# The half-sized products' first accumulator in two parts: one 512-column matmul for both operand parts, and PSUM pools by phase

## The chip, the cores and the metric

The kernel runs on one core of a Trainium2 chip. The time is the device time of one execution in microseconds; below, "before" is the kernel without the change.

## What is computed

A decoder trunk of two layers over one sequence of 512 tokens with 1024 features, in float32: a feed-forward layer (FFN), a mixer and a second FFN in each layer. The change touches the four FFNs alone. Each is a SwiGLU of 2816 columns behind an RMS norm:

```python
def swiglu(h, w13, w2):
    gate, up = jnp.split(h @ w13, 2, axis=-1)
    return (jax.nn.silu(gate) * up) @ w2
for l in range(DEPTH):
    x = x + 0.5 * swiglu(rms_norm(x, ffn1_norm[l]), ffn1_w13[l], ffn1_w2[l])
    ...
    x = x + 0.5 * swiglu(rms_norm(x, ffn2_norm[l]), ffn2_w13[l], ffn2_w2[l])
```

## The kernel before

**Data.** The activations are kept with features on the 128 partitions and the 512 tokens along the free dimension. Every float32 operand of TensorE is split in two parts of a narrower type, `hi` and `lo`; a product is the sum of three matmuls, `hi·xh`, `hi·xl` and `lo·xh` (L388 to L390), with the weights stationary. A weight block is loaded by DMA (`w_raw`, or `w_a` for a block and `w_s` for a sum of blocks), ACT casts its high part (`w_hi`, L85), and DVE subtracts for the low part (`w_lo`, L89).

**One FFN** (`ffn`, L353). The 22 column tiles of gate and up are done in thirds of 8, 8 and 6 tiles (`THIRDS`). The first tiles of a call (6, 4, 0 and 4 in the four calls, `PLAIN`) are plain products of 512 columns; the others are taken two at a time by `pair` (L370), 37 pairs in all. After each third come its "down" products `pd`, eight groups of 24 (or 18) matmuls of 512 columns, which read the pair's results `ah` and `al`.

**A pair** is a 2 by 2 block product of gate and up tiles against two halves of 256 tokens, done with seven half-sized products instead of eight. The operands' combinations of token halves are made before (`hh`, `hl`: seven forms each, high and low part); the weights' sums `s1` to `s4` are added by DVE (L114). The seven products f0 to f6 go one after the other into three PSUM banks, X, Z and Y, which are drained on the way:

- f0 into X, copied to `e[:, 0]` by ACT (L391)
- f1 into Z, added by DVE (L397)
- f2 into X on top of f0, copied to `e[:, 1]` by ACT (L395)
- f3 into Y, copied to `e[:, 2]` by ACT (L393)
- f4 into X, subtracted by DVE (L399)
- f5 into Y, subtracted by DVE (L401)
- f6 into X; ACT applies silu to it straight from PSUM (L404), DVE multiplies (L406)

So X is written four times in a pair, and each time the PE may go on writing it only when the drain of the time before is done. Each product is 24 matmuls of 256 columns: 2 column halves, 4 blocks of features, 3 parts. The silu of the other three quarters is L403, their multiplication L405; L411 (ACT) and L412 (DVE) split the result into `ah` and `al`.

**Order.** The program is recorded with a scheduler that fixes each engine's order ahead of time; every engine then takes its instructions strictly in that order, and waits at an instruction whose operands are late. Within an FFN `w_hi` and `w_lo` have five buffers each: the parts of a product's weights can be made only when PE has finished with the product five places before. All PSUM tiles come from one pool of eight banks, `psum` (L161). `mm` (L200) issues each matmul.

## Time and profile before

| | us |
|---|---|
| median of 3 runs (1862.65 to 1864.32) | 1862.82 |
| the profiled execution | 1862.41 |
| its span, first to last instruction | 1860.7 |
| TensorE busy | 1836.7 (99%) |
| VectorE (DVE) busy | 1357.0 (73%) |
| ScalarE (ACT) busy | 919.2 (49%) |

The profiled execution lies 0.4 us under the median. The span is the profiled time less 1.7 us that lie around it. Busy shares are averages over the whole program; what limits a stage is read from that stage alone. A row of the timeline gives an instruction's start and its duration; instructions of one engine overlap, so the distance between two starts (the pitch) is what one costs the engine, and the duration is what a waiting engine sees. A row of the groups by line gives the busy time, the mean duration in ns, and the idle time before the instructions with what ended it.

### The profile page before, as it was taken

What the parts mean: (1) busy time and instruction counts of PE and PEld (TensorE: products, weight loads), DVE (VectorE), ACT (ScalarE), POOL (GpSimd) and SP (SyncE); (2) the same over time, 40 slices, a digit from 0 to 9 for tenths busy, and PEclk for the clock granted to TensorE, in tenths of its full rate; (3) what the DMA queues carried; (4) which work ended last, traced back from release to release, by engine and by line L of the source; (5) the groups of instructions that cost most, each with busy time, mean ns of one, the idle gap of its engine ahead of it and who ended that gap; (6) DMA issues with size and microseconds to landing.
All of it is one profiled execution on the core that took longest, in us unless ns stands there. A gap on an engine that the chain in (4) does not pass through costs nothing. (4 is left out here: it accounts for less than half of the span.)

```text
span 1860.7 us, 27263 instructions
## 1 busy us (share of the span) xinstructions
PE 1836.7 (99%) x11040; PEld 1628.6 (88%) x11040; DVE 1357.0 (73%) x1678; ACT 919.2 (49%) x1282; POOL 123.5 (7%) x165
## 2 busy tenths in 40 slices
PE   9999999999999999999999999999999999999999
PEld 7889989787789899897789999898776789899897
DVE  8958757698878486576799667575799779577483
ACT  6525425477555254354555335254588655345251
POOL 1000000032000000000100000000345300000000
PEclk9999999999999999999999999999999999999999
DMA  6223523222414134232463324234476421425131
GB/s 227 89 81 93 146 63 108 69 91 79 151 54 157 50 112 136 67 104 79 159 204 122 111 86 138 66 105 145 124 197 165 140 88 59 144 74 159 54 111 59
DMA packets 73117, 207.87 MB, mean 112 GB/s; under 512 B 7584, under 2 KB 17056, under 8 KB 72480
## 3 DMA queue, kind: packets, MB, share of 16 engines
q1 hardware_dynamic: 72704, 205.81, 36.2%
q8 instruction: 86, 1.41, 0.3%
q10 hardware_dynamic: 288, 0.32, 0.1%
q14 instruction: 39, 0.32, 0.0%
HBM read 189.85 MB, written 16.25 MB: 111 GB/s over the span
## 5 line engine op out<-in xcount | busy, mean ns | idle before, releaser
L85 ACT CAST w_hi<-w_raw 128x1024 fp32r<-128x1024 f32 (+1 forms) x165 | 165.7, 1007 | 270.3 <-PE pdffn L201 82.4
L85 ACT CAST w_hi<-w_s 128x1024 fp32r<-128x1024 f32 x148 | 155.2, 1050 | 246.5 <-PE pdffn L201 105.4
L89 DVE TENSOR_TENSOR w_lo<-w_raw,w_hi 128x1024 fp32r<-128x1024 f32 (+3 forms) x191 | 218.1, 1145 | 71.8 <-ACT w_hi L85 65.7
L201 PE MATMUL pXffn<-hhffn,w_hi 128*128 128x256 f32 x832 | 235.8, 283 | 0.3 <-ACT effn L391 0.3
L201 PE MATMUL pXffn<-hhffn,w_lo 128*128 128x256 f32 x832 | 235.6, 283 | 0.0
L201 PE MATMUL pXffn<-hlffn,w_hi 128*128 128x256 f32 x832 | 235.6, 283 | 0.0
L201 PE MATMUL pdffn<-ahffn,w_hi 128*128 128x512 f32 x592 | 230.9, 390 | 0.3
L201 PE MATMUL pdffn<-alffn,w_hi 128*128 128x512 f32 x592 | 230.8, 390 | 0.0
L201 PE MATMUL pdffn<-ahffn,w_lo 128*128 128x512 f32 x592 | 230.5, 389 | 0.0
L89 DVE TENSOR_TENSOR w_lo<-w_s,w_hi 128x1024 fp32r<-128x1024 f32 x148 | 180.7, 1222 | 32.3 <-ACT w_hi L85 31.9
L85 ACT CAST w_hi<-w_a 128x1024 fp32r<-128x1024 f32 x111 | 116.6, 1050 | 167.5 <-PE pdffn L201 70.2
L89 DVE TENSOR_TENSOR w_lo<-w_a,w_hi 128x1024 fp32r<-128x1024 f32 x111 | 135.6, 1222 | 36.1 <-ACT w_hi L85 36.0
L201 PEld LDWEIGHTS pXffn<-hhffn,w_hi 128*128 128x128 f32 x832 | 159.8, 192 | 1.1 <-ACT effn L391 0.7
L201 PEld LDWEIGHTS pXffn<-hlffn,w_hi 128*128 128x128 f32 x832 | 159.8, 192 | 0.3
L201 PEld LDWEIGHTS pXffn<-hhffn,w_lo 128*128 128x128 f32 x832 | 159.8, 192 | 0.0
L455 DVE SCALAR_TENSOR_TENSOR x<-pdffn,x 128x512 f32<-128x512 f32 x72 | 49.8, 691 | 141.2 <-PE pdffn L201 141.2
L201 PEld LDWEIGHTS pdffn<-ahffn,w_hi 128*128 128x128 f32 x592 | 111.2, 188 | 24.6 <-ACT ahffn L411 1.8
L201 PEld LDWEIGHTS pdffn<-alffn,w_hi 128*128 128x128 f32 x592 | 111.2, 188 | 24.2 <-DVE alffn L412 1.1
L201 PEld LDWEIGHTS pdffn<-ahffn,w_lo 128*128 128x128 f32 x592 | 111.2, 188 | 22.7
L201 PE MATMUL pYffn<-hhffn,w_lo 128*128 128x256 f32 x416 | 117.8, 283 | 0.0
L201 PE MATMUL pYffn<-hhffn,w_hi 128*128 128x256 f32 x416 | 117.8, 283 | 0.0
L201 PE MATMUL pYffn<-hlffn,w_hi 128*128 128x256 f32 x416 | 117.8, 283 | 0.0
(1146 smaller groups left out, 4631.4 us busy)
## 6 DMA issues: line engine op xcount, KB each, us to landing
w_a<-in_ffn_s SPq DMA_DIRECT2D x148, 512.0 KB, 3.7
w_raw<-in_ffn_w SPq DMA_DIRECT2D x90, 512.0 KB, 4.5
w_raw<-in_ffn_w SPq DMA_DIRECT2D x32, 384.0 KB, 3.3
w_raw<-in_w_in SPq DMA_DIRECT2D x16, 512.0 KB, 3.6
qp<-qd SPq DMA_DIRECT2D x14, 512.0 KB, 6.1
w_raw<-in_w_out SPq DMA_DIRECT2D x8, 512.0 KB, 3.7
w_raw<-in_w_k SPq DMA_DIRECT2D x8, 512.0 KB, 3.6
w_raw<-in_w_v SPq DMA_DIRECT2D x8, 512.0 KB, 3.7
```

Of the source, the lines that this page charges most:

```text
L85: nc.scalar.copy(out=hi[:, cs], in_=raw[:, cs])
L89: eng.tensor_tensor(out=lo[:, cs], in0=raw[:, cs], in1=hi[:, cs].bitcast(F32), op=ALU.subtract)
L201: return nc.tensor.matmul(o, l, r, start=start, stop=stop, skip_group_check=True)
L455: nc.vector.scalar_tensor_tensor(out=x[m], in0=pd, scalar=0.5, in1=x[m], op0=ALU.mult, op1=ALU.add)
```

## The change

For each feature block and column half the X products take `hi·xh` and `hi·xl` in one matmul of 512 columns: the moving operand is two pieces of 256, and `hh` becomes one tile that holds high and low part (`[P, 2, 7, 256]`). Their results stand side by side, so X is now two banks, one for each column half, with a high and a low part of 256 columns that have yet to be added; `lo·xh` still goes, in 256 columns, onto the high part. Z and Y stay as they were. The drains of X change with it:

- f0 and f2: ACT copies the low part (L384 of the changed kernel), then DVE adds the high part (L385); before, one ACT copy
- f4: two DVE operations (L425, L426); before, one
- f6: ACT negates the low part into `e` (L430), DVE takes the high part off (L431), and silu (L434) and product (L436) read SBUF; before, they read PSUM

PSUM pools are opened by phase: in an FFN four single banks and two two-bank tiles for X (`ps=4, px=2`), elsewhere eight single banks. The plain products' gate and up share a two-bank tile for every other column tile.

```diff
-    pp = ctx.enter_context(tc.tile_pool(name="pp", bufs=8, space=PSUM))
...
-        return pp.tile([P, S], F32, tag="ps", name=name)
-
-
-    cur = SimpleNamespace(stack=[], names=[])
+        return cur.pp.tile([P, S], F32, tag="ps", name=name)
+
+    def psum2(name):
+
+        return cur.pp.tile([P, 2, S], F32, tag="px", name=name)
+
+    def open_psum(name, **bufs):
+
+        if cur.pp is not None:
+            cur.pp.pool_ctx.__exit__(None, None, None)
+        ctxm = tc.tile_pool(name=name, bufs=2, space=PSUM, reuse_waits="tile")
+        cur.pp = Pool(ctxm.__enter__(), bufs)
+        cur.pp.pool_ctx = ctxm
...
-        hi = cur.ht.tile([P, 7, HS], F32R, tag="hh", name=f"hh{name}{j}")
-        lo = cur.ht.tile([P, 7, HS], F32R, tag="hl", name=f"hl{name}{j}")
+        t = cur.ht.tile([P, 2, 7, HS], F32R, tag="hh", name=f"hh{name}{j}")
+        hi, lo = t[:, 0], t[:, 1]
...
+        open_psum(f"pf{n}{l}", ps=4, px=2)
...
+        def add2(o, p, q):
+            nc.scalar.copy(out=o, in_=q)
+            nc.vector.tensor_tensor(out=o, in0=p, in1=o, op=ALU.add)
...
-                    banks[bank] = psum(f"p{bank}{n}{l}{i}")
+                    banks[bank] = (psum2 if bank == "X" else psum)(f"p{bank}{n}{l}{i}")
                 ps = banks[bank]
+                if bank == "X":
+                    xh, xl = (ps[:, :, k * HS:(k + 1) * HS] for k in range(2))
                 for c in range(2):
-                    o = ps[:, c * HS:(c + 1) * HS]
+                    o = ps[:, c] if bank == "X" else ps[:, c * HS:(c + 1) * HS]
                     for j in range(KT // 2):
                         ws = slice(c * S + j * P, c * S + j * P + P)
-                        xh, xl = hn[j][0][:, form], hn[j][1][:, form]
-
-                        mm(o, hi[:, ws], xh, new and c == 0 and j == 0, False)
-                        mm(o, hi[:, ws], xl, False, False)
-                        mm(o, lo[:, ws], xh, False, j == KT // 2 - 1)
-
+                        if bank == "X":
+                            mm(o, hi[:, ws], hn[j][:, :, form], new and j == 0, False)
+                            mm(o[:, 0:HS], lo[:, ws], hn[j][:, 0, form], False, j == KT // 2 - 1)
+                            continue
+                        th, tl = hn[j][:, 0, form], hn[j][:, 1, form]
+
+                        mm(o, hi[:, ws], th, new and c == 0 and j == 0, False)
+                        mm(o, hi[:, ws], tl, False, False)
+                        mm(o, lo[:, ws], th, False, j == KT // 2 - 1)
...
                if f == 0:
-                    nc.scalar.copy(out=e[:, 0], in_=ps)
+                    add2(in2[0], xh, xl)
+                elif f == 1:
+                    nc.vector.tensor_tensor(out=c11, in0=ps, in1=c11, op=ALU.add)
+                elif f == 2:
+                    add2(in2[1], xh, xl)
                 elif f == 3:
-                    nc.scalar.copy(out=e[:, 2], in_=ps)
-                elif f == 2:
-                    nc.scalar.copy(out=e[:, 1], in_=ps)
-                elif f == 1:
-                    nc.vector.tensor_tensor(out=e[:, 0], in0=ps, in1=e[:, 0], op=ALU.add)
+                    nc.scalar.copy(out=c22, in_=ps)
                 elif f == 4:
-                    nc.vector.tensor_tensor(out=e[:, 2], in0=ps, in1=e[:, 2], op=ALU.subtract)
+                    nc.vector.tensor_tensor(out=in2[2], in0=xh, in1=in2[2], op=ALU.subtract)
+                    nc.vector.tensor_tensor(out=in2[2], in0=xl, in1=in2[2], op=ALU.add)
                 elif f == 5:
-                    nc.vector.tensor_tensor(out=e[:, 1], in0=ps, in1=e[:, 1], op=ALU.subtract)
-            ps = banks["X"]
-            nc.scalar.activation(out=e[:, 0:3, 0:HS], in_=e[:, 0:3, 0:HS], func=AF.Silu)
-            last_silu.append(nc.scalar.activation(out=e[:, 3, 0:HS], in_=ps[:, 0:HS], func=AF.Silu, scale=-1.0))
-            nc.vector.tensor_tensor(out=e[:, 0:3, 0:HS], in0=e[:, 0:3, 0:HS], in1=e[:, 0:3, HS:S], op=ALU.mult)
-            nc.vector.scalar_tensor_tensor(out=e[:, 3, 0:HS], in0=ps[:, HS:S], scalar=-1.0, in1=e[:, 3, 0:HS], op0=ALU.mult, op1=ALU.mult)
+                    nc.vector.tensor_tensor(out=c21, in0=ps, in1=c21, op=ALU.subtract)
+                elif f == 6:
+                    nc.scalar.mul(in2[3], xl, -1.0)
+                    nc.vector.scalar_tensor_tensor(out=in2[3], in0=xh, scalar=-1.0, in1=in2[3], op0=ALU.mult, op1=ALU.add)
+
+            for b in (slice(0, 3), slice(3, 4)):
+                last_silu.append(nc.scalar.activation(out=e[:, b, 0:HS], in_=e[:, b, 0:HS], func=AF.Silu))
+            for b in (slice(0, 3), slice(3, 4)):
+                nc.vector.tensor_tensor(out=e[:, b, 0:HS], in0=e[:, b, 0:HS], in1=e[:, b, HS:S], op=ALU.mult)
...
-                pg, pu = psum(f"pg{n}{l}{i}"), psum(f"pu{n}{l}{i}")
+                if i % 2 == 0:
+                    pgu = psum2(f"pgu{n}{l}{i}")
+                    pg, pu = pgu[:, 0], pgu[:, 1]
+                else:
+                    pg, pu = psum(f"pg{n}{l}{i}"), psum(f"pu{n}{l}{i}")
```

The lines of the operations move: the copy of f3 is L423 after the change, the drains of f1 and f5 L419 and L428, the splits L441 and L442, `mm` L213.

**Where the order moves on PE.** In the names, `effn1018` is the drained tile of the pair of column tiles 18 and 19 in the first FFN, call 0 (`ffn1`, `0`, `18`); `pXffn1020` is bank X of the pair behind it. Before, PE goes from f1 of pair 1020 (Z) straight to f2 (X):

```order
L201 MATMUL pZffn1020_2965<-hhffn103_420,w_lo78_2827 128x256
L201 MATMUL pXffn1020_2935<-hhffn100_365,w_hi79_2859 128x256
L201 MATMUL pXffn1020_2935<-hlffn100_366,w_hi79_2859 128x256
L201 MATMUL pXffn1020_2935<-hhffn100_365,w_lo79_2860 128x256
L201 MATMUL pXffn1020_2935<-hhffn101_380,w_hi79_2859 128x256
L201 MATMUL pXffn1020_2935<-hlffn101_381,w_hi79_2859 128x256
```

After the change, at the same place:

```order
L213 MATMUL pZffn1020_2766<-hhffn103_420,w_lo78_2648 128x256
L213 MATMUL pYffn1020_2822<-hhffn100_368,w_hi80_2704 128x256 x2
L213 MATMUL pYffn1020_2822<-hhffn100_368,w_lo80_2705 128x256
L213 MATMUL pYffn1020_2822<-hhffn101_382,w_hi80_2704 128x256
L213 MATMUL pXffn1020_2743<-hhffn100_368,w_hi79_2673 128x512
L213 MATMUL pXffn1020_2743<-hhffn100_368,w_lo79_2674 128x256
L213 MATMUL pXffn1020_2743<-hhffn101_382,w_hi79_2673 128x512
L213 MATMUL pXffn1020_2743<-hhffn101_382,w_lo79_2674 128x256
L213 MATMUL pXffn1020_2743<-hhffn102_406,w_hi79_2673 128x512
```

Four matmuls of f3 (Y; a row with x2 is two) now stand between f1 and f2, and f2 takes two matmuls for a feature block and column half where it took three. Of the sixteen matmuls of the next pair's f0, six stand further ahead, between the products f3 to f6 of pair 1018 (five in f3's place, behind 20 of its 24, and one before f6), so that ten are left between f6 and Z; before, all of f0 stood there. In the first pair of a stage Z is followed by one matmul of f3 instead of four.

**Where the order moves on DVE.** The end of pair 1018 and the beginning of pair 1020, before:

```order
L89 TENSOR_TENSOR w_lo80_2891<-w_s3_80_2888,w_hi80_2890 128x1024
L405 TENSOR_TENSOR effn1018_2696<-effn1018_2696 128x3x256
L89 TENSOR_TENSOR w_lo81_2932<-w_s1_79_2855,w_hi81_2931 128x1024
L406 SCALAR_TENSOR_TENSOR effn1018_2696<-pXffn1018_2701,effn1018_2696 128x256
L412 TENSOR_TENSOR alffn1018_2923<-effn1018_2696,ahffn1018_2922 128x512
L412 TENSOR_TENSOR alffn1019_2927<-effn1018_2696,ahffn1019_2926 128x512
L89 TENSOR_TENSOR w_lo82_2962<-w_a22_77_2792,w_hi82_2961 128x1024
L397 TENSOR_TENSOR effn1020_2930<-pZffn1020_2965,effn1020_2930 128x512
```

And after the change:

```order
L436 TENSOR_TENSOR effn1018_2531<-effn1018_2531 128x3x256
L89 TENSOR_TENSOR w_lo81_2740<-w_s1_79_2669,w_hi81_2739 128x1024
L431 SCALAR_TENSOR_TENSOR effn1018_2531<-pXffn1018_2536,effn1018_2531 128x512
L89 TENSOR_TENSOR w_lo82_2763<-w_a22_77_2613,w_hi82_2762 128x1024
L436 TENSOR_TENSOR effn1018_2531<-effn1018_2531 128x256
L385 TENSOR_TENSOR effn1020_2738<-pXffn1020_2743,effn1020_2738 128x512
L442 TENSOR_TENSOR alffn1018_2731<-effn1018_2531,ahffn1018_2730 128x512
L442 TENSOR_TENSOR alffn1019_2735<-effn1018_2531,ahffn1019_2734 128x512
L419 TENSOR_TENSOR effn1020_2738<-pZffn1020_2766,effn1020_2738 128x512
```

The drain of f6 (L431) now stands between two weight parts, the product of the last quarter (L436) behind both, and the drain of f0 of the next pair (L385), which was not on DVE before, behind all of them; the splits (L412, now L442) come after it.

**And the middle of the pair, DVE after the change:**

```order
L114 TENSOR_TENSOR w_s1_79_2669<-w_a21_77_2611,w_a22_77_2613 128x1024
L89 TENSOR_TENSOR w_lo77_2618<-w_a11_77_2609,w_hi77_2617 128x1024
L385 TENSOR_TENSOR effn1018_2531<-pXffn1018_2536,effn1018_2531 128x512
L114 TENSOR_TENSOR w_s2_79_2671<-w_s1_79_2669,w_a11_77_2609 128x1024
L89 TENSOR_TENSOR w_lo78_2648<-w_a12_77_2615,w_hi78_2647 128x1024
L114 TENSOR_TENSOR w_s3_80_2702<-w_a11_77_2609,w_a21_77_2611 128x1024
L425 TENSOR_TENSOR effn1018_2531<-pXffn1018_2536,effn1018_2531 128x512
L114 TENSOR_TENSOR w_s4_83_2792<-w_s2_79_2671,w_a12_77_2615 128x1024
L426 TENSOR_TENSOR effn1018_2531<-pXffn1018_2536,effn1018_2531 128x512
L89 TENSOR_TENSOR w_lo79_2674<-w_s2_79_2671,w_hi79_2673 128x1024
```

The drain of f2 (L385) stands behind `w_lo77`, and the two of f4 (L425, L426) have a weight sum between them.

**And the first pair behind plain products** (column tiles 4 and 5 of `ffn2`, call 0), DVE after the change:

```order
L89 TENSOR_TENSOR w_lo132_4851<-w_s1_130_4778,w_hi132_4850 128x1024
L380 TENSOR_TENSOR effn203_4840<-effn203_4840 128x512
L385 TENSOR_TENSOR effn204_4849<-pXffn204_4854,effn204_4849 128x512
L89 TENSOR_TENSOR w_lo133_4874<-w_a22_128_4707,w_hi133_4873 128x1024
L339 TENSOR_TENSOR affn203l_4846<-effn203_4840,affn203h_4845 128x512
L419 TENSOR_TENSOR effn204_4849<-pZffn204_4877,effn204_4849 128x512
L114 TENSOR_TENSOR w_s4_134_4903<-w_s2_130_4780,w_a12_128_4709 128x1024
L89 TENSOR_TENSOR w_lo135_4936<-w_a11_135_4927,w_hi135_4935 128x1024
L89 TENSOR_TENSOR w_lo134_4906<-w_s4_134_4903,w_hi134_4905 128x1024
L385 TENSOR_TENSOR effn204_4849<-pXffn204_4854,effn204_4849 128x512
```

L380 multiplies gate and up of the plain tile 3, and L339 splits it; the drain of f0 (L385) stands behind the first and that of f1 (L419) behind the second. f0's was ACT's before, and PE's f2 waited for it; now 15 matmuls of f3 stand ahead of f2.

## Rows read from the trace of the kernel before

**Rows 1.** The page: busy time of each engine, granted clock in 40 slices.

```profile
PE 1836.7 (99%) x11040; PEld 1628.6 (88%) x11040; DVE 1357.0 (73%) x1678; ACT 919.2 (49%) x1282; POOL 123.5 (7%) x165
...
PEclk9999999999999999999999999999999999999999
```

**Rows 2.** Stretches of the pair stages: busy time (instructions) of each engine.

```profile
core 0: us, PE busy (x) PEld busy (x) DVE busy (x) ACT busy (x) POOL busy (x), PEclk, DMA share, GB/s
...
562.60:603.70 41.10, 40.79 (x337) 40.37 (x336) 35.84 (x40) 23.04 (x30) 0.00 (x0) 1.00 0.50 168
647.30:727.90 80.60, 80.60 (x673) 80.60 (x672) 63.45 (x66) 42.13 (x53) 0.00 (x0) 1.00 0.45 131
...
sum 746.40, PE 746.09 PEld 745.58 DVE 591.81 ACT 395.61 POOL 0.00; mean PE 62.17 PEld 62.13 DVE 49.32 ACT 32.97 POOL 0.00
```

**Rows 3.** Timeline of PE: plain products of 512 columns, then the first pair's X.

```profile
73.11 0.39 PE L201 MATMUL puffn<-h_7h,w_hi 128*128 128x512 f32 x1
...
73.79 0.28 PE L201 MATMUL pXffn<-hhffn,w_hi 128*128 128x256 f32 x1
...
76.66 0.28 PE L201 MATMUL pZffn<-hhffn,w_hi 128*128 128x256 f32 x1
```

**Rows 4.** Timeline of PE around the end of an X product, in a later pair.

```profile
1107.12 0.28 PE L201 MATMUL pXffn<-hhn,w_lo 128*128 128x256 f32 x1
1107.24 0.28 PE L201 MATMUL pXffn<-hhn,w_hi 128*128 128x256 f32 x1
```

**Rows 5.** Timeline of ACT, the same place.

```profile
1107.37 1.05 ACT L85 CAST w_hi<-w_s 128x1024 fp32r<-128x1024 f32 x1 [1.09 <-PE pXffn L201]
1108.32 0.38 ACT L404 ACTIVATE effn<-pXffn 128x256 f32<-128x256 f32 x1
```

**Rows 6.** Timeline of DVE, the same place.

```profile
1108.45 1.23 DVE L89 TENSOR_TENSOR w_lo<-w_s,w_hi 128x1024 fp32r<-128x1024 f32 x1 [0.79 <-ACT w_hi L85]
1109.59 0.42 DVE L406 SCALAR_TENSOR_TENSOR effn<-pXffn,effn 128x256 f32<-128x256 f32 x1
```

**Rows 7.** Timeline of DVE: an operation of 512 columns from PSUM and the next.

```profile
562.13 0.68 DVE L366 TENSOR_TENSOR effn<-puffn,rs_n 128x512 f32<-128x512 f32 x1
562.73 1.22 DVE L89 TENSOR_TENSOR w_lo<-w_s,w_hi 128x1024 fp32r<-128x1024 f32 x1
```

**Rows 8.** Timeline of DVE: the first pair of a stage of two.

```profile
569.67 0.69 DVE L367 TENSOR_TENSOR effn<-effn 128x512 f32<-128x512 f32 x1
...
572.01 0.69 DVE L397 TENSOR_TENSOR effn<-pZffn,effn 128x512 f32<-128x512 f32 x1
...
587.11 0.42 DVE L406 SCALAR_TENSOR_TENSOR effn<-pXffn,effn 128x256 f32<-128x256 f32 x1
587.44 1.22 DVE L89 TENSOR_TENSOR w_lo<-w_s,w_hi 128x1024 fp32r<-128x1024 f32 x1
```

**Rows 9.** Timeline of PE at the wait of the same stage.

```profile
568.24 0.28 PE L201 MATMUL pZffn<-hhffn,w_lo 128*128 128x256 f32 x1
568.77 0.39 PE L201 MATMUL pXffn<-hhffn,w_hi 128*128 128x256 f32 x1 [0.25 <-ACT effn L391]
568.99 0.28 PE L201 MATMUL pXffn<-hlffn,w_hi 128*128 128x256 f32 x1
```

**Rows 10.** Timeline of PE's weight loads at that wait.

```profile
568.12 0.19 PEld L201 LDWEIGHTS pZffn<-hhffn,w_lo 128*128 128x128 f32 x1
568.76 0.19 PEld L201 LDWEIGHTS pXffn<-hhffn,w_hi 128*128 128x128 f32 x1 [0.45 <-ACT effn L391]
```

**Rows 11.** Timeline of ACT at that wait.

```profile
568.15 0.56 ACT L391 COPY effn<-pXffn 128x512 f32<-128x512 f32 x1
```

**Rows 12.** Groups by line: the drain of f4.

```profile
L399 DVE TENSOR_TENSOR effn<-pXffn,effn 128x512 f32<-128x512 f32 x37 | 25.4, 687 | 9.1 <-PE pXffn L201 9.0
```

**Rows 13.** Timeline of PE in the attention: matmuls with an operand in two pieces.

```profile
1377.01 0.28 PE L201 MATMUL z<-sph,ntri 128*128 128x256 f32 x1
1377.13 0.28 PE L201 MATMUL z<-spl,ntri 128*128 128x256 f32 x1
```

More of the change, by code (lines that the diff above doesn't have):

```diff
@@ L157, in trunk @@
     wp = ctx.enter_context(tc.tile_pool(name="wp", bufs=3))
-    pp = ctx.enter_context(tc.tile_pool(name="pp", bufs=8, space=PSUM))
     dp = ctx.enter_context(tc.tile_pool(name="dp", bufs=8, space=DRAM))
     def psum(name):
-        return pp.tile([P, S], F32, tag="ps", name=name)
-    cur = SimpleNamespace(stack=[], names=[])
+        return cur.pp.tile([P, S], F32, tag="ps", name=name)
[7 more added lines that the diff above has]
+        cur.pp.pool_ctx = ctxm
+    cur = SimpleNamespace(stack=[], names=[], pp=None)
     def temp(tag, name, dt=F32, bufs=2, shape=None):
@@ L190, in phase_ffn @@
         close_pools()
-        cur.ht = open_pool("ht", hh=4, hl=4)
+        cur.ht = open_pool("ht", hh=4)
         cur.ep = open_pool("ep", e=2)
@@ L196, in phase_mix @@
         close_pools()
+        open_psum(f"pm{len(cur.names)}", ps=8)
         cur.hp = open_pool("hp", bh=8, bl=8, ch=8, cl=8)
@@ L350, in normed @@
         nc.vector.scalar_tensor_tensor(out=lo[:, 6], in0=b22, scalar=-1.0, in1=hi[:, 6].bitcast(F32), op0=ALU.mult, op1=ALU.subtract)
-        return hi, lo
+        return t
     def ffn(n, l, ht, g, rs, after, full=False, hn=None):
+        open_psum(f"pf{n}{l}", ps=4, px=2)
         r, queue, nf = None, [], PLAIN[n, l]
@@ new lines, in pair @@
+                        th, tl = hn[j][:, 0, form], hn[j][:, 1, form]
+                        mm(o, hi[:, ws], th, new and c == 0 and j == 0, False)
+                        mm(o, hi[:, ws], tl, False, False)
+                        mm(o, lo[:, ws], th, False, j == KT // 2 - 1)
+                c11, c21, c22, c12 = (e[:, k] for k in range(4))
+                in2 = [t.rearrange("p (c t) -> p c t", c=2) for t in (c11, c21, c22, c12)]
+                if f == 0:
+                    add2(in2[0], xh, xl)
[3 more added lines that the diff above has]
+                    add2(in2[1], xh, xl)
+                elif f == 3:
+                    nc.scalar.copy(out=c22, in_=ps)
@@ L462, in x_tiles @@
         return halves, [halves[m // 4][:, m % 4] for m in range(KT)]
+    open_psum("pw", ps=1)
     x2, x = x_tiles("x")
@@ L662, in trunk @@
     cur.tp = open_pool("tk")
+    open_psum("pk", ps=8)
     r3 = None
@@ L1017, in trunk @@
     ffn("ffn2", 1, h5, G_FFN2[1], n5.rstd, lambda m, t: nc.sync.dma_start(out[:, m], t))
+    cur.pp.pool_ctx.__exit__(None, None, None)
     close_pools()
```

## The prediction

> **What bounds the kernel now.** I began with the page: PE is busy for 1836.7 of 1860.7 us at full granted clock, DVE for 73% [rows 1]. That names PE, but a share over the program hides stages, so the stretches of the pair stages come next. There PE never stops: 746.09 of 746.40 us, and in a stage of four pairs 80.60 of 80.60, with DVE at 63.45 [rows 2]. The one kind with waits is the stage of two pairs behind plain products, 41.10 us [rows 2] where two pairs of 168 matmuls need 40.3: 0.8 of waits. So PE's own time bounds a pair, and what saves matmul time saves time as long as no wait takes its place. The third view, the timelines, gives prices: on PE for the matmuls, on ACT and DVE for the drains that PE will wait for.
>
> **What is saved.** A 512-column matmul costs (73.79 - 73.11) / 3 = 0.2267 us [rows 3]. A 256-column one costs 80.60 / 672 = 0.1199 [rows 2], and the first X product agrees: 24 in 76.66 - 73.79 = 2.87 [rows 3]. Merging two saves 2 x 0.1199 - 0.2267 = 0.013. There are 37 pairs x 4 X products x 8 = 1184 such merges: **15.6 us**, 0.42 per pair (20.15 becomes 19.73). An X product falls from 2.88 to 2.77.
>
> **What is added.** On DVE four operations of 128x512 per pair (L385 twice, the second of f4, L431 in place of nothing). One costs 0.60 in a row of others [rows 7], so 2.4 us per pair. A pair has 11 operations of 128x1024 at 1.14 [rows 6], three drains at 0.60, 0.87 + 0.33 for the two products (the second from [rows 8]) and two splits at 0.60: 16.7 us, now 19.1 of some 19.9. DVE still has room, but little, so what counts is the place of each drain in its strict order. On ACT one copy more per pair lies in idle time (42.13 of 80.60 busy, [rows 2]): nothing.
>
> **The length of a drain.** Call T the moment at which the next matmul could start after an X product. The last matmul of a product starts at 1107.12, so T is 1107.24 [rows 4]. The cast of the freed weight buffer starts at T + 0.13, and the next ACT operation 0.95 later [rows 5]. Its w_lo starts at T + 1.21 and the DVE operation behind it at T + 2.35 [rows 6]. A drain put there takes 0.69 [rows 12] and some 0.05 until PE knows (a copy ends at 568.15 + 0.56 = 568.71 [rows 11], PE loads at 568.76 [rows 10]). So a drain behind one w_lo releases PE at **T + 3.09**.
>
> A late release costs more than its lateness. At the wait that before has, X could have started at 568.24 + 0.12 = 568.36 and started at 568.77; its next matmul came 0.22 later instead of 0.12 [rows 9]. I charge each restart 0.10, and a release less than 0.10 ahead of its matmul the difference.
>
> On this the Trainium skill speaks too. "TensorE: Matmul & The Clock Gate", section "Step-by-step: what each phase is for", says that PE pulls weight loads ahead of running matmuls. By that rule a restart would find its weights loaded and cost nothing, which would take some 4 us off the waits below (about 45 restarts). The trace disagrees at this place: the load starts with the release, 0.64 after the load ahead of it [rows 10].
>
> **Place by place**, with the order shown above:
>
> 1. *f0 of a later pair, before f2.* DVE takes w_lo81 at T + 1.21 (T: end of the pair before), L431 to 2.95, w_lo82 to 4.09, L436 to 4.42, then the drain: 4.42 + 0.69 + 0.05 = T + 5.16. PE has ten matmuls of f0 (1.73), 24 of Z (2.88), four of Y (0.48): T + 5.09. Cost 0.07 + 0.10 = 0.17. 37 pairs less 12 first ones less two priced in 4: 23 x 0.17 = 3.9.
> 2. *f0 of a first pair.* T + 3.09 against Z and one Y, 3.00: 0.19. Nine stages of three or four pairs: 1.7.
> 3. *f2 and f4 elsewhere.* In a middle pair f2's drain is released at 3.09 against 20 matmuls of Y and five of f0, 3.32: no cost. f4's second drain stands behind s4: 0.20 + 0.60 + 1.14 + 0.69 + 0.05 = 2.68 against 3.00: none. In four of the nine first pairs a w_lo stands between f4's two drains, 3.09 again against 3.00 to 3.1, and f2's is just in time: 0.28 together; in the other five some 0.1. The last pair of a third of six tiles has one filler instead of five: 0.1 in each of four. Sum 1.1 + 0.5 + 0.4 = 2.0.
> 4. *The two stages behind plain products.* DVE is late there: f1's add starts at 572.01, Z's last matmul at 568.24 [rows 8, 9]. f0's drain now stands behind L380, that is at 569.67 + 0.60 = 570.27 [rows 8], and releases at 571.01; PE gets there at 568.25 + 15 x 0.12 = 570.05. Cost 1.06. The matmuls of the next pair's f0 that are pulled ahead then wait for their w_hi (T + 0.13 + 1.05 + 0.05 of f2) and w_lo: 0.25 and 1.02. With 0.4 in the second pair 2.7, less the 0.8 that is there now: 1.9 each, 3.8.
> 5. *Matmuls that wait for weights in the middle of a pair*: a w_lo is there at T + 1.21 + 1.22 + 0.05 = 2.48 against 20 x 0.12 + 0.23 = 2.63. Nothing, with 0.15 to spare. The pools by phase and the shared gate and up tile change no wait in a pair; cover is the whole phase before. Nothing.
>
> Sum of waits 3.9 + 1.7 + 2.0 + 3.8 = **11.4**, against 15.6: net -4.2. From the profiled execution 1862.4 that is 1858.2; the median of the runs stands 0.4 higher, so 1858.6, **1859 us**.
>
> The sum is a difference of near equals. The unknown prices: a DVE add that reads two banks in pieces has no row. From below it is the row I take, 0.60 and 0.69 [rows 7, 12]; nothing excludes a little more, so from above I take the 0.42 that 256 columns cost [rows 8] twice, 0.84. I take the lower, since the data are the same size. The merged matmul is bounded below by 0.2267 and above by two single ones, 0.24; I take the lower, by the nearest row: in the attention, matmuls of 2 x 128 columns from an operand in two pieces start 0.12 apart [rows 13], as contiguous ones do.
>
> **Rivals.**
>
> *All drains are hidden* (chance 0.22). Place 1 lacks only 0.17 of 5.1 us; if DVE's steps are 3% shorter, or the release comes as soon as the drain's write does, places 1 to 3 vanish and 1862.4 - 15.6 + 3.8 = 1851 is left, 1847 if the backlog does no harm either. (Were the restarts alone free, 1859 - 4 = 1855, inside the forecast's own band.) For it: PE waits for nothing now. Against: the steps were measured without gaps.
>
> *DVE becomes the bound* (0.22), the one that ends slower. Place: f0's drain, then f2's and f4's. If an add costs 0.75 instead of 0.60, six of them put DVE at 20.0 us a pair, place 1 grows by 0.3, and the spare 0.13 to 0.2 of f2, f4 and the pulled-ahead w_lo is gone: some 0.3 to 0.4 more in each of 37 pairs, 11 to 15 us, 1870 to 1874. It decides from about 0.1 us more per add, where place 1 alone eats what is left of the saving.
>
> *An operand in two pieces is slow* (0.06). If the merged matmul took 0.24, the saving would be 0 and the waits some 8 (covers are longer): 1871. [Rows 13] speak against it. [...]
>
> *It cancels* (0.08): the waits take all of the 15.6, as they do where each release is 0.1 later than I have it; 1860 to 1865.
>
> **Numbers.** My forecast has 0.42. 0.2%, 3.7 us, is about what a measurement of this kernel can tell from no change, so faster means below 1859.1. The forecast, 1854 to 1864, is split there: 0.24 faster, 0.18 same. With 0.22 of the first rival, faster is 0.45; same is 0.18 + 0.08 and a little of the rivals' edges, 0.28; slower 0.22 + 0.06 less those edges, 0.27. The range takes in the first rival down to 1849 and the slow ones up to 1873.
>
> **What would show it.** 9856 matmuls; X products at 2.77 from start to start; idle PE time before X with DVE's L385 as its releaser, about 0.1 to 0.2 each in later pairs, 1 us at the two stages behind plain products; DVE at 19 of 20 in a pair. Stages of four pairs should take 79.6 to 80.0 us instead of 80.60. Wrong would be idle PE before f4 or f6 in middle pairs, L385 longer than 0.7, or a pitch of 0.24 in the merged matmuls.

## The result, and the profile after

| | before | after |
|---|---|---|
| median, us (3 runs of before from above and one more beside the change; 4 runs of after) | 1863.57 | 1873.37 |
| lowest and highest | 1862.65 to 1865.53 | 1872.99 to 1874.07 |
| ratio with its 95% interval | | 1.0054 [1.0041, 1.0066] |
| the profiled execution, and its span | 1862.41, 1860.7 | 1874.07, 1872.2 |

The change makes the kernel slower by 9.8 us. The forecast, 1859 and rather faster, has the wrong sign, and the time lies 0.4 us above the range.

Page of after: busy time of each engine, granted clock in 40 slices. These answer to [rows 1].

```profile
PE 1840.5 (98%) x9856; PEld 1567.0 (84%) x9856; DVE 1442.0 (77%) x1826; ACT 941.9 (50%) x1319; POOL 122.6 (7%) x165
...
PEclk9999999999999999999999999999999999999999
```

The 9856 matmuls are the forecast's, 1184 fewer. PE's busy time rose by 3.8 us all the same, and DVE's by 85. A page's averages cannot say where 11.5 us of span went, so I compared the start of each pair stage in the two traces. After minus before, in us: -0.1, -0.1, -0.2 in the first FFN call; +0.6, +2.8, +2.8 in the second; +7.6, +9.4, +9.4 in the third; +10.8, +11.4, +11.4 in the fourth; +11.5 at the end. The stages of four and three pairs with their down products cost what they cost before. The time is lost in the two stages behind plain products (2.2 and 0.6), in the mixers that precede three calls (0.8, 4.8 and 1.4), and in the first stage of the third call (1.8). The third call's beginning alone holds 6.6 of the 11.5. The 0.8 and the 1.4 are not shown to come from the change: in the mixers ahead of the second and the fourth call PE stood at about half clock for 7.1 us in this execution and for some 3.6 us in that of before.

Stretches of after's pair stages, columns as in [rows 2]: the stage of two, one of four, the first stage of the third call, and the sum of all twelve.

```profile
563.20:606.30 43.10, 40.81 (x273) 37.09 (x272) 40.13 (x47) 23.81 (x31) 0.00 (x0) 1.00 0.50 166
650.10:731.20 81.10, 81.10 (x549) 74.40 (x548) 71.87 (x81) 43.98 (x56) 0.00 (x0) 1.00 0.41 130
...
970.50:1053.40 82.90, 82.73 (x547) 75.80 (x548) 70.80 (x80) 44.20 (x56) 0.00 (x0) 0.98 0.43 138
...
sum 754.70, PE 751.91 PEld 689.12 DVE 662.98 ACT 407.17 POOL 0.00; mean PE 62.66 PEld 57.43 DVE 55.25 ACT 33.93 POOL 0.00
```

The stretch of the stage of four holds three matmuls of the down product, 0.7 us; the stage itself takes about 80.4, where before took 80.60 and the forecast was 79.6 to 80.0. PE is busy throughout, though it waits: the durations of pipelined matmuls overlap, and a wait of 0.1 to 0.2 us disappears under them. Such waits are read from starts. The timeline of PE where f0 of a later pair ends its wait (place 1 of the forecast):

```profile
998.56 0.28 PE L213 MATMUL pYffn<-hhn,w_hi 128*128 128x256 f32 x1
998.70 0.50 PE L213 MATMUL pXffn<-hhn,w_hi 128*128 128x512 f32 x1
999.04 0.28 PE L213 MATMUL pXffn<-hhn,w_lo 128*128 128x256 f32 x1
999.15 0.40 PE L213 MATMUL pXffn<-hhn,w_hi 128*128 128x512 f32 x1
...
1001.27 0.40 PE L213 MATMUL pXffn<-hhn,w_hi 128*128 128x512 f32 x1
```

And DVE there:

```profile
997.63 0.42 DVE L436 TENSOR_TENSOR effn<-effn 128x256 f32<-128x256 f32 x1
997.96 0.68 DVE L385 TENSOR_TENSOR effn<-pXffn,effn 128x512 f32<-128x512 f32 x1
```

The drain ends at 997.96 + 0.68 = 998.64 and f2 starts at 998.70, 0.14 behind the matmul ahead of it where 0.12 is usual. The next start comes 0.34 later, where it is 0.24 elsewhere: the restart's 0.10, as forecast. From 999.15 to 1001.27 lie six turns of a 512- and a 256-column matmul: 0.353 each. The forecast had 0.2267 + 0.1199 = 0.347, and three single matmuls cost 0.360.

The beginning of the third call is another matter. PE there:

```profile
963.82 0.39 PE L213 MATMUL v<-w_hi,n3a7l 128*128 128x512 f32 x1
970.48 0.76 PE L213 MATMUL pXffn<-hhn,w_hi 128*128 128x512 f32 x1 [6.28 <-DVE vl L775]
971.04 0.41 PE L213 MATMUL pXffn<-hhn,w_lo 128*128 128x256 f32 x1
971.26 0.63 PE L213 MATMUL pXffn<-hhn,w_hi 128*128 128x512 f32 x1
...
971.90 0.63 PE L213 MATMUL pXffn<-hhn,w_hi 128*128 128x512 f32 x1
```

DVE there:

```profile
969.59 0.75 DVE L775 SCALAR_TENSOR_TENSOR vl<-v,rc,vh 128x512 fp32r<-128x512 f32 x1 [0.22 <-DMA vd<-vl]
970.25 1.21 DVE L114 TENSOR_TENSOR w_s<-w_s,w_a 128x1024 f32<-128x1024 f32 x1
976.21 1.23 DVE L114 TENSOR_TENSOR w_s<-w_a,w_a 128x1024 f32<-128x1024 f32 x1 [4.74 <-DMA w_a<-in_ffn_s]
977.35 0.69 DVE L385 TENSOR_TENSOR effn<-pXffn,effn 128x512 f32<-128x512 f32 x1
```

And after's stretches before, behind and after that wait (PEclk is the third column from the end):

```profile
955.00:970.40 15.40, 9.21 (x41) 7.30 (x39) 15.18 (x18) 7.15 (x10) 0.00 (x0) 0.89 0.83 236
970.40:974.00 3.60, 3.52 (x11) 3.06 (x12) 1.07 (x1) 0.00 (x0) 0.00 (x0) 0.52 1.07 327
974.00:978.00 4.00, 3.92 (x31) 3.59 (x29) 1.79 (x3) 1.69 (x3) 0.00 (x0) 1.00 0.20 79
```

The first X of the call waits 6.28 us for `vl`, the last operation that reads a V tile of the mixer. Then PE runs at the lower of its levels (0.52 granted, 1.2 GHz) for some 3.6 us: a 512 with its 256 takes 0.64 (971.26 to 971.90) instead of 0.353. Before, X followed the mixer's last matmul directly, at full clock. The allocation tells why: the call's first X lies in banks 0 and 1, and bank 1 holds the V tile that is drained last; before, it got bank 5, whose V tile had been drained long ago.

### The profile page after: what moved, and what is told of

The parts are those of the page before. It is cut to its first block, busy times and chain, and to the rows that moved or that the text cites. A ratio compares the mean times of both kernels' runs of the same rounds, so it can differ in the third digit from the quotient of the medians.

```text
span 1872.2 us, 25180 instructions
## 1 busy us (share of the span) xinstructions
PE 1840.5 (98%) x9856; PEld 1567.0 (84%) x9856; DVE 1442.0 (77%) x1826; ACT 941.9 (50%) x1319; POOL 122.6 (7%) x165
## 4 chain that ended last, share of the span: by engine, by line
PE 63%; DVE 10%; issue 4%; ACT 2%; POOL 1%; DMA 1%; POOLq 0%; SPq 0%; DVEq 0%; ACTq 0%
PE pdffn L213 18%; PE pXffn L213 17%; PE pYffn L213 9%; PE pZffn L213 4%; PE k L213 2%; PE wo L213 2%; PE wout L213 2%; DVE w_lo L89 2%; PE pguffn L213 1%; PE z L213 1%; PE q L213 1%; PE rec L213 1%; PE puffn L213 1%; PE pgffn L213 1%; DVE sp L886 1%
## 5 line engine op out<-in xcount | busy, mean ns | idle before, releaser
L213 PE MATMUL pXffn<-hhffn,w_hi 128*128 128x512 f32 x832 | 298.9, 401 | 1.2 <-ACT affn203h L338 0.9
L213 PE MATMUL pXffn<-hhffn,w_lo 128*128 128x256 f32 x832 | 232.3, 281 | 0.8 <-DVE w_lo L89 0.8
L213 PE MATMUL pdffn<-ahffn,w_hi 128*128 128x512 f32 x592 | 231.5, 392 | 0.0
L213 PE MATMUL pdffn<-alffn,w_hi 128*128 128x512 f32 x592 | 230.7, 390 | 0.0
L213 PE MATMUL pdffn<-ahffn,w_lo 128*128 128x512 f32 x592 | 230.3, 389 | 0.0
L213 PEld LDWEIGHTS pXffn<-hhffn,w_hi 128*128 128x128 f32 x832 | 155.8, 188 | 39.7 <-DVE effn L385 2.0
L213 PEld LDWEIGHTS pXffn<-hhffn,w_lo 128*128 128x128 f32 x832 | 157.1, 189 | 2.6 <-DVE w_lo L89 1.3
L213 PE MATMUL pYffn<-hhffn,w_hi 128*128 128x256 f32 x832 | 155.6, 283 | 0.7 <-ACT effn L423 0.7
L213 PE MATMUL pXffn<-hhn,w_hi 128*128 128x512 f32 x352 | 127.8, 405 | 6.4 <-DVE vl L775 6.3
L213 PEld LDWEIGHTS pYffn<-hhffn,w_hi 128*128 128x128 f32 x832 | 130.4, 190 | 3.4 <-ACT effn L423 1.1
L213 PEld LDWEIGHTS pdffn<-ahffn,w_hi 128*128 128x128 f32 x592 | 111.0, 188 | 26.4 <-ACT ahffn L441 4.1
L213 PEld LDWEIGHTS pdffn<-alffn,w_hi 128*128 128x128 f32 x592 | 111.1, 188 | 25.0 <-DVE alffn L442 2.4
L213 PEld LDWEIGHTS pdffn<-ahffn,w_lo 128*128 128x128 f32 x592 | 111.2, 188 | 22.1
L213 PE MATMUL pYffn<-hhffn,w_lo 128*128 128x256 f32 x416 | 117.6, 283 | 0.0
L213 PE MATMUL pXffn<-hhn,w_lo 128*128 128x256 f32 x352 | 98.9, 282 | 0.0
```

The source lines that it names most:

```text
L213: return nc.tensor.matmul(o, l, r, start=start, stop=stop, skip_group_check=True)
```

## The experiments

The sessions had their own runs of before (medians 1863.19, 1863.33, 1863.74 and 1863.40); each ratio below is against those of its session. First theory: the pools by phase cost some 7 us at the third call, the merged matmul's pitch 5, the drains' waits the 11 forecast. Rivals: the operand in two pieces, DVE's load.

**e1: operand in one piece.** The parts of a form lie side by side.

```diff
-        t = cur.ht.tile([P, 2, 7, HS], F32R, ...
-        hi, lo = t[:, 0], t[:, 1]
+        t = cur.ht.tile([P, 7, 2, HS], F32R, ...
+        hi, lo = t[:, :, 0], t[:, :, 1]
-    mm(o, hi[:, ws], hn[j][:, :, form], ...
+    mm(o, hi[:, ws], hn[j][:, form].rearrange("p c t -> p (c t)"), ...
```

> The changed kernel with the operand's high and low part side by side for each form, so that the merged matmul reads one piece of 512 columns instead of two of 256; nothing else differs, and PE's order is the same. Theory A (two pieces cost time): in the changed kernel a merged matmul and its 256-column neighbour take 234.7 + 116.9 = 351.6 ns from start to start, where 227 + 120 = 347 had been forecast; with one piece they fall to 347 and 1184 x 4.6 ns = 5.5 us go: 1868. Rival B (the turn from 512 to 256 columns and back costs it, whatever the operand's layout): the pair stays at 351 to 352 ns and the time at 1873.

Measured 1874.31, 1.0058 [1.0046, 1.0071], the same as after. The starts of merged matmuls stand 234.6 ns from the next and those of their 256-column neighbours 116.9; in after 234.7 and 116.9. The two pieces cost nothing.

**e2: other banks for the call's first X.** Z and a spare are taken ahead of X, so X gets banks 4 and 5.

```diff
+        if nf == 0:
+            first = [psum(f"pZ{n}{l}0"), psum(f"spare{n}{l}")]
-    banks[bank] = (psum2 if bank == "X" else psum)(...)
+    banks[bank] = first[0] if nf == 0 and i == 0 and bank == "Z" else (psum2 if bank == "X" else psum)(...)
```

> The changed kernel, with the two single-bank tiles of the third FFN call taken before its first X tile, so that X lands in banks 4 and 5, which the V products of the phase before left long ago, instead of 0 and 1, where the last V tile is still to be drained. Theory A (the pools by phase cost a wait there): the 6.3 us of idle PE before that X go, and the 3.5 us at half clock behind it too: about 7 us, 1866. Rival B (DVE is late there anyway, so the wait only moves to the next tile of the pair): 1872 or more, with idle PE before Z or f2 of the same pair.

Measured 1875.00, 1.0063 [1.0049, 1.0077]: no gain. The first X no longer waits, but f2 does, by PE's timeline:

```profile
978.11 0.79 PE L213 MATMUL pXffn<-hhn,w_hi 128*128 128x512 f32 x1 [8.45 <-DVE effn L387]
```

Its releaser (L387 is this kernel's L385) stands on DVE behind a weight sum that waits for a load, at 976.23 as in after at 976.21. The banks were one of two causes.

**e3: before with nothing but the pools by phase** (and the shared gate and up tile; X takes half of a two-bank tile).

```diff
-    pp = ctx.enter_context(tc.tile_pool(name="pp", bufs=8, space=PSUM))
+        open_psum(f"pf{n}{l}", ps=4, px=2)
+        open_psum(f"pm{len(cur.names)}", ps=8)
-    banks[bank] = psum(f"p{bank}{n}{l}{i}")
+    banks[bank] = psum2(f"pX{n}{l}{i}")[:, 0] if bank == "X" else psum(f"p{bank}{n}{l}{i}")
```

> The kernel before with the PSUM pools by phase alone: X has a two-bank tile of which one bank is used, plain gate and up share a two-bank tile as in the change; products and drains are those of before. Theory A (the pools' banks make the boundary wait): idle PE of about 6 us before the first X of the third FFN call, half clock behind it, and 6 to 8 us more than before: 1870. Rival B (the wait comes from DVE's later order in the changed kernel): no such idle time, 1863 to 1864.

Measured 1871.09, 1.0041 [1.0029, 1.0054]. PE's timeline at the third call:

```profile
961.67 0.39 PE L213 MATMUL v<-w_hi,n3a7l 128*128 128x512 f32 x1
968.42 0.55 PE L213 MATMUL pXffn<-hhn,w_hi 128*128 128x256 f32 x1 [6.36 <-DVE vl L758]
```

And its stretch behind the wait:

```profile
968.40:972.00 3.60, 3.58 (x17) 3.60 (x18) 1.00 (x1) 0.00 (x0) 0.00 (x0) 0.50 1.09 357
```

With seven half-products exactly as before, the wait, the lower clock and most of the loss are there: the mixer ahead of the call takes 5.1 us more, its first stage 2.5, and every other pair stage stands within 0.3 of before. The pools are the main cause.

**e4: the low part never added.** X is still two banks, but its high part alone is drained, as before.

```diff
-                    add2(in2[0], xh, xl)
+                    nc.scalar.copy(out=in2[0], in_=xh)
-                    nc.vector.tensor_tensor(out=in2[2], in0=xl, in1=in2[2], op=ALU.add)
```

> The changed kernel without the second half of each X drain: the low part's 256 columns are multiplied but never added (the product of the weights' high part and the operand's low part is left out of four of the seven products), f0 and f2 are drained by one ACT copy, f4 by one DVE operation, f6 by silu straight from PSUM, as before. Theory A (the two-step drains make some 50 small waits in the pair stages, 11 us in all): the waits go but for those that before has, 1863 to 1865, and DVE is busy 90 us less. Rival B (the pair stages lose little by waits; the lost time is the merged matmul's pitch and the boundary): 1870 to 1873.

Measured 1861.86, 0.9990 [0.9981, 0.9999]. The same stretch of a stage of four as above, in this kernel:

```profile
644.80:724.60 79.80, 79.80 (x546) 73.83 (x546) 63.46 (x66) 42.18 (x53) 0.00 (x0) 1.00 0.42 132
```

DVE is back at 63.46. With its down products the stage takes 123.0 us, 0.9 less than in after; of the 1.3 between the two stretches, 0.7 are the down matmuls in after's. The wait at the third call is still there (6.62 us). So the added drains cost 1873.37 - 1861.86 = 11.5 us (11.9 by the ratios, each against its own session), against the 11.4 that the forecast charged for them.

**e6: the drains off DVE's order.** For f0 and f2 one ACT copy takes both parts into two quarters of `e`; DVE adds in SBUF, and PE waits for ACT alone.

```diff
-            nc.scalar.copy(out=o, in_=q)
-            nc.vector.tensor_tensor(out=o, in0=p, in1=o, op=ALU.add)
+            nc.scalar.copy(out=e[:, a:b + 1:b - a].rearrange(...), in_=ps.rearrange(...))
+            nc.vector.tensor_tensor(out=e[:, a], in0=e[:, a], in1=e[:, b], op=ALU.add)
```

> The changed kernel with f0 and f2 drained by one ACT copy of both parts into two quarters of the tile, so that PE may write X again after ACT; DVE adds the parts from SBUF afterwards. DVE has as many operations as in the changed kernel. Theory A (the place of these two drains in DVE's order makes most of the pair stages' waits): the pair stages fall to the length that they have without the low parts' drains, but for f4's two steps: 8 to 10 us less, 1864 to 1866, with the idle time at the third FFN call still there. Rival B (DVE's load is what costs, wherever the adds stand): the stages stay, 1872 or more.

Measured 1865.59, 1.0012 [1.0003, 1.0021]. A stage of four:

```profile
647.20:726.90 79.70, 79.70 (x546) 73.80 (x545) 71.64 (x81) 47.44 (x56) 0.00 (x0) 1.00 0.40 132
```

DVE is as busy as in after (71.64 and 71.87), and the stage is as short as without the adds (e4). DVE's load is not the bound; the place of the drain in its order is.

**e7: the merged matmuls of a column half in a row,** four of 512 columns, then four of 256.

```diff
                         if bank == "X":
                             mm(o, hi[:, ws], hn[j][:, :, form], new and j == 0, False)
-                            mm(o[:, 0:HS], lo[:, ws], hn[j][:, 0, form], False, j == KT // 2 - 1)
                             continue
+                    for j in range(KT // 2 if bank == "X" else 0):
+                        mm(o[:, 0:HS], lo[:, c * S + j * P:c * S + j * P + P], hn[j][:, 0, form], ...
```

> The changed kernel with the X products' matmuls in another order: for a column half first the four of 512 columns, then the four of 256, instead of in turn. Theory A (it is the turn between 512 and 256 columns with its weight loads that makes 351.6 ns of 347; one piece instead of two changed nothing): with a quarter of the turns most of the 4.6 ns go, some 4 us: 1869. Rival B (a matmul of 512 columns beside weight loads of 128 columns for one of 256 costs the same in any order): 351 to 352 ns for a pair, 1873 to 1875.

Measured 1870.60, 1.0036 [1.0022, 1.0050]; the interval overlaps after's. Start to start: 232.4 ns between merged matmuls, 229.4 from the last of them, 118.0 between the others and 118.4 from the last of these: 349.7 for a 512 with its 256, or 1.9 ns less than in after. That is 2.2 us in 1184, and the medians are 2.8 apart. Taking turns is a part of the pitch; whether the time follows is inconclusive.

**e8 and e9: e6 with e2's banks, and that with e7's rows.** Their edits are those above together.

> ACT's copy of both parts for f0 and f2, and X of the third FFN call in banks 4 and 5. With the banks alone the wait there only moved, from the first X to f2 of the same pair, which waited 8.7 us for the DVE drain of f0 that stood behind weight sums whose loads were late. Theory A (two causes behind one another: the banks, and a drain on DVE): together they remove it, no idle PE there and no half clock, 7 to 8 us below the run with ACT's copy alone: 1857 to 1859, below the kernel before. Rival B (a third wait for the late loads stands behind both): 1863 or more, with idle PE in that pair.

> As the run with ACT's copies and the banks, with the 512- and 256-column matmuls of X grouped. Theory A (turns): some 4 us less than that run, 1853 to 1855. Rival B: the same time.

Measured 1864.76, 1.0008 [1.0000, 1.0017], and 1864.71, 1.0003 [0.9994, 1.0012]: hardly better than e6. In e9 a 512 with its 256 takes 350.1 ns and in e8 352.4, and the time is the same, so e7's gain in time stays unshown. The wait moved again, now to f2, whose ACT copy waits for DVE's add of f0 behind the same late sum; this is read from e8's profiled execution, which at 1869.40 is the slowest of its eleven.

**e10: e3 with e2's banks,** to see that second cause without the change's drains.

> The kernel before with the pools by phase, and X of the third FFN call in banks 4 and 5. Theory A (pools alone cost only through the banks of that first X; f0's drain is a copy on ACT here and does not stand behind the late weight sums): no idle PE there, 1863 to 1864, like the kernel before. Rival B (pools by phase cost in another way too, or the wait moves as it did in the changed kernel): 1867 or more.

Measured 1869.92, 1.0035 [1.0023, 1.0048], as slow as e3. The idle time is now before Y, by PE's timeline:

```profile
982.55 0.58 PE L213 MATMUL pYffn<-hhn,w_hi 128*128 128x256 f32 x1 [5.34 <-ACT effn L408]
```

ACT's timeline ahead of it:

```profile
980.97 1.04 ACT L85 CAST w_hi<-w_a 128x1024 fp32r<-128x1024 f32 x1 [8.02 <-DMA w_a<-in_ffn_s]
981.92 0.58 ACT L408 COPY effn<-pYffn 128x512 f32<-128x512 f32 x1
```

DVE's timeline in this kernel:

```profile
968.86 1.22 DVE L114 TENSOR_TENSOR w_s<-w_s,w_a 128x1024 f32<-128x1024 f32 x1
975.14 1.23 DVE L114 TENSOR_TENSOR w_s<-w_a,w_a 128x1024 f32<-128x1024 f32 x1 [5.07 <-DMA w_a<-in_ffn_s]
976.29 1.22 DVE L89 TENSOR_TENSOR w_lo<-w_a,w_hi 128x1024 fp32r<-128x1024 f32 x1
...
978.56 0.69 DVE L412 TENSOR_TENSOR effn<-pZffn,effn 128x512 f32<-128x512 f32 x1
```

And SyncE's queue:

```profile
977.53 0.34 SPq L109 DMA_DIRECT2D w_a<-in_ffn_s  x1
```

The same place in the kernel before:

```profile
969.22 1.22 DVE L89 TENSOR_TENSOR w_lo<-w_a,w_hi 128x1024 fp32r<-128x1024 f32 x1
970.35 0.68 DVE L397 TENSOR_TENSOR effn<-pZffn,effn 128x512 f32<-128x512 f32 x1
...
975.56 1.22 DVE L114 TENSOR_TENSOR w_s<-w_a,w_a 128x1024 f32<-128x1024 f32 x1
```

ACT's timeline there, before:

```profile
974.57 0.59 ACT L393 COPY effn<-pYffn 128x512 f32<-128x512 f32 x1 [0.37 <-PE pYffn L201]
977.01 1.06 ACT L85 CAST w_hi<-w_a 128x1024 fp32r<-128x1024 f32 x1 [1.85 <-DMA w_a<-in_ffn_s]
```

With other pools the scheduler put the weight sum for the next pair, whose load lands at about 975, ahead of a weight part (`w_lo`) and of the drain of f1. Before, it stands behind both, and by its turn the load has landed. Y does not wait for that drain but for ACT's copy of f3, and the way there is longer. The weight part is the last reader of a weight buffer, so behind the late sum it ends at 976.29 + 1.22 = 977.51 and the next load into that buffer is issued at 977.53. ACT's cast of that load stands ahead of the copy of f3, so it starts at 980.97, the copy at 981.92 and Y at 982.55. Before, the copy stands ahead of that cast. Two orders differ, then, DVE's and ACT's.

**e11, e12, e13: are the loads late because of their queue?** The stores of V go through GpSimd's queue instead of SyncE's: in e12 with e2, in e11 with e2 and ACT copies into a scratch tile (diff at f4), in e13 with before.

```diff
-    nc.sync.dma_start(vt[e, :, :, s, :], ...
+    nc.gpsimd.dma_start(vt[e, :, :, s, :], ...
```

> The changed kernel with the banks, with f0 and f2 drained by two ACT copies (the low part into a scratch tile of its own, so that f2's copy need not wait for DVE's add of f0), and with the V results stored through GpSimd's DMA queue, so that the weight loads of the third FFN call's second pair need not stand behind these stores in SP's queue. Theory A (three causes behind one another at that place: banks, a drain on DVE or waiting for DVE, loads late behind the stores): no idle PE of over 1 us there, pair stages as with ACT's copy: 1856 to 1859. Rival B (loads are late for want of buffers, not for the queue): 1862 or more, idle PE in that pair.

> The changed kernel with the banks and with the V results stored through GpSimd's queue; drains as in the change. Theory A (queue): the 8.7 us of idle PE before f2 go, and what is left are the small waits of the pair stages against a saving of 10 us: 1865 to 1867. Rival B (buffers): 1873 to 1875, as with the banks alone.

> The kernel before with the V results stored through GpSimd's queue: a control for the two runs with it. PE does not wait there before, so by either theory 1862 to 1864; anything else is the queue's own effect.

Measured: e11 1867.17, 1.0017 [1.0008, 1.0026]; e12 1879.35, 1.0081 [1.0068, 1.0094], with 10.06 us of idle before f2; e13 1865.85, 1.0011 [1.0002, 1.0020]. The queue costs some 2 us by itself and the loads come no sooner. The theory of the queue falls. In the 20 us around this place the DMA share is 0.73 to 0.99 in before as well, so these loads have little room. What they wait for is a buffer: in e10 loads are issued at 970.10 and 977.53, just behind the DVE operations that end at 970.08 and 977.51 (968.86 and 976.29, 1.22 each). More weight buffers were not tried.

**f1 and f2: the order put back.** In the third call's first pair the sums are held behind the drain of f1, by a dependence that issues nothing. f1 has e3's pools and e2's banks, f2 the pools alone.

```diff
+            i = self.nc.vector.tensor_tensor(out=g[name], in0=p, in1=q, op=ALU.add)
+            if self.hold:
+                self.hold(i)
...
+    W.hold = lambda s, d=dr: tc.add_manual_dep(s.ins, d.ins.name, NOSYNC, ...)
```

> The kernel before with the pools by phase, X of the third FFN call in banks 4 and 5, and the weight sums of that call's second pair held behind f1's drain in DVE's order, where they stood before the pools. Theory A (the pools cost in two ways at one place: the bank, and an order on DVE that puts a sum whose loads come late ahead of the drains): no idle PE there, 1863 to 1865. Rival B (still another cause): 1868 or more.

> The kernel before with the pools by phase and the sums held behind f1's drain, X left in the banks of the last V tile. Theory A (each of the two causes is enough by itself): X waits for the last V tile's drain, 5 to 6.5 us idle and half clock behind it, 1869 to 1871, as with the pools alone. Rival B (the order on DVE is the whole cause, and with it mended the V tile is drained in time): 1863 to 1866.

Measured: f1 1865.47, 1.0009 [1.0001, 1.0018]; f2 1872.03, 1.0038 [1.0024, 1.0052]. PE's timeline in f2:

```profile
969.60 0.55 PE L215 MATMUL pXffn<-hhn,w_hi 128*128 128x256 f32 x1 [6.34 <-DVE vl L764]
```

The banks alone (e10) give back nothing that counts, the order alone (f2) nothing, both (f1) nearly all: each cause is enough by itself to leave PE idle for 5 to 6 us. In f1 the load behind the weight part is issued at 971.50, 6 us sooner than in e10. What is left are waits of 0.4, 1.0 and 1.7 us in that pair; the 1.0 is Y's, for ACT's cast still stands ahead of the copy of f3.

**f3 and f4: the changed kernel with both.** f3 is after with e2's banks and the sums behind the drain of f2; f4 has the copies on ACT besides:

```diff
+            s = cur.ep.tile([P, 2, HS], F32, tag="xs", name=f"xs{n}{l}")
+            nc.scalar.copy(out=s, in_=q)
+            nc.scalar.copy(out=o, in_=p)
+            nc.vector.tensor_tensor(out=o, in0=o, in1=s, op=ALU.add)
```

> The changed kernel with both mended: X of the third call in banks 4 and 5, and the sums of its second pair held behind f2's drain. Theory A (of the 10 us that the change costs, 7 to 8 are the pools at that place): no idle PE over 1 us there, 1865 to 1867; what is left of the loss is that the small waits of the pair stages outweigh the saving of the merge. Rival B (the wait moves again): 1872 or more.

> As the run before this, with f0 and f2 drained by two ACT copies, the low part into a scratch tile, and the sum of both by DVE from SBUF. Theory A (both losses mended): the pair stages as with ACT's copy, no wait at the third call: 1856 to 1859, below the kernel before. Rival B: 1863 or more, with idle PE in that pair or in others.

Measured: f3 1873.00, 1.0046 [1.0033, 1.0058], no better than after, since f2 still waits 3.20 us for DVE and the lower clock follows; holding the sums there is not enough while the drain itself is on DVE. f4 1860.06, **0.9977 [0.9967, 0.9987]**: faster than both kernels, and just above the 1856 to 1859 expected. Its stages:

```profile
646.20:725.80 79.60, 79.60 (x546) 73.69 (x545) 71.64 (x81) 47.94 (x64) 0.00 (x0) 1.00 0.38 133
959.80:1041.90 82.10, 80.22 (x545) 73.80 (x545) 76.95 (x87) 51.61 (x69) 0.00 (x0) 1.00 0.49 162
```

The stage of four takes 1.0 us less than before, and the third call's first stage runs at full clock with 1.88 us of idle left.

## Why the prediction was wrong

- **Place 5, "The pools by phase and the shared gate and up tile change no wait in a pair; cover is the whole phase before. Nothing."** This step failed, and it decides the sign. e3 gives its price: 7.9 us (1871.09 against 1863.19). I took for cover the phase before, but PE runs from the mixer's last V product into f0 without a gap, so what matters is which bank X gets and how late that bank's last reader is: 6.28 us of idle, then 3.6 us at half the clock. And I read the order on DVE inside pairs only; at the third call's start the new pools also moved a sum with a late load ahead of a weight part that frees a buffer. The next load, ACT's cast of it and the copy of f3 behind that cast then came late, and this costs nearly as much by itself (e10, 6.2 us above its session's before).
- **"What is saved."** The count, 1184, was right; the term was mis-sized. A merged matmul and its neighbour take 351.6 ns from start to start (waits left out), where 346.6 was forecast, so a merge saves 360 - 351.6 = 8.4 ns, and 1184 of them 9.9 us instead of 15.6. The 0.2267 is from matmuls of 512 columns among their like [rows 3]; those that alternate with 256 take 0.2347, 8.0 ns more, of which the neighbours give 3.0 back. The pieces are not why (e1), taking turns explains 1.9 ns of the 5.0 by the pitch (e7), and the rest is open. In e4, where PE hardly waits, the two take 352.9, which makes it 7.1 ns and 8.4 us.
- **The sum of the waits, 11.4.** Right: 11.5 to 11.9 by e4. From the stages: without the third call's first stage they and their down products grew by 2.1 us, and 33 pairs saved 33 x 0.269 = 8.9, so they wait 11.0. Place 1 shows it in one row, at 998.70. Place 4 was right in kind and unequal in size: the two stages lose 2.2 + 0.54 = 2.7 and 0.6 + 0.54 = 1.1 net, where 1.9 each was forecast. The forecast took the 0.8 of waits in before off both, but only the first had them: the second, in the fourth call, took 40.30 us before, with PE busy throughout. PE's timeline in the first of them:

```profile
570.56 0.28 PE L213 MATMUL pYffn<-hhffn,w_lo 128*128 128x256 f32 x1
571.70 0.47 PE L213 MATMUL pXffn<-hhffn,w_hi 128*128 128x512 f32 x1 [0.86 <-ACT affn203h L338]
...
575.78 0.51 PE L213 MATMUL pXffn<-hhffn,w_hi 128*128 128x512 f32 x1
577.04 0.39 PE L213 MATMUL pXffn<-hhffn,w_lo 128*128 128x256 f32 x1 [0.75 <-DVE w_lo L89]
...
597.66 0.50 PE L213 MATMUL pYffn<-hhffn,w_hi 128*128 128x256 f32 x2 [0.68 <-ACT effn L423]
```

  The first is the forecast's wait of f2: it could have started at 570.56 + 0.12 and started 1.02 later (forecast 1.06). The profile names ACT's L338, which ends at 571.61, but what f2 needs by the code is DVE's L385, which ends at 571.55. The second is the pulled-ahead f0 that waits for its `w_lo`: 577.04 less 575.78 and a pitch of 0.24 is 1.02, forecast 1.02. The third, 0.8 in the second pair behind ACT's copy of f3, was not in the forecast.
- **The restart, 0.10.** Held (998.70 to 999.04). The Trainium skill, "TensorE: Matmul & The Clock Gate", section "Step-by-step: what each phase is for", would have the next weights loaded by then; the weight load of that matmul starts at 998.70 with it, so here too the trace disagrees.
- **Length of the adds.** The lower bound was right. Groups by line of after:

```profile
L385 DVE TENSOR_TENSOR effn<-pXffn,effn 128x512 f32<-128x512 f32 x74 | 50.5, 683 | 0.0
...
L426 DVE TENSOR_TENSOR effn<-pXffn,effn 128x512 f32<-128x512 f32 x37 | 25.3, 684 | 0.3
```

  Reading two banks in pieces takes 683 ns, one bank 687 before [rows 12].
- **The rivals.** "DVE becomes the bound" named 1870 to 1874, where the time fell, but its mechanism is not this one: its condition, adds of 0.75, is refuted by L385, and e6 has the same DVE load without the loss. "An operand in two pieces is slow" is refuted by e1. Merged matmuls start 234.7 ns apart with two pieces and 234.6 with one. "All drains are hidden" is what e6 and f4 make of the kernel by hand; the drains' waits in after are real.

In sum, saving and waits nearly cancel (8.4 to 9.9 against 11.0 to 11.9). By the larger saving the forecast's net gain of 4.2 was 5.7 too high there, and what it priced at nothing cost 7.9: together 13.6 of the 14.4 by which it missed. The remaining 0.8 is no more than the 0.8 and 1.4 of the other two mixers, which are not tied to the change.

## What to carry to other kernels

When a change opens or splits PSUM pools, ask at every boundary which bank the next phase's first accumulator gets and when that bank's last reader is done: waits of 3.2 to 8.5 us there were followed by a stretch at half clock, while the two waits of f4, 1.01 and 0.87 us, were not. Read the order on each strict engine at those boundaries too, not only where the edit is; one step that waits for a load holds up the drains behind it, and the weight parts too, and with them the next loads and what other engines do with these. And where a drain only frees a bank, look for an engine that has no late work ahead of it at that place, even if that adds a pass: in f4, ACT's copies turned 0.5% of loss into 0.2% of gain.

## What the runs showed of the hardware

- After 6.28 us of idle PE was granted 0.52 of its clock for 3.6 us (after), then 1.00. After 6.36 us (e3) it had 0.50 from 968.4 to 973 and 1.00 from 974, after 5.34 us (e10) 0.50 from 982.5 to 985, 0.55 on to 989 and then 1.00, so the length differs. The Trainium skill, "TensorE: Matmul & The Clock Gate", section "What's actually happening", names two levels of 1.2 and 2.4 GHz; the rows agree.
- A 512-column matmul costs 226.7 ns among its like, 232.4 in rows of four, 234.7 in turns with 256 columns, whose own cost falls from 119.9 to 116.9 there. I had not expected a matmul's price to depend on its neighbours.
